# A hybrid layer step: the samples' attention emitted in parts among the last prompt attention blocks

## The chip, the cores and the metric

The kernel runs on one core of one Trainium2 chip. The metric is the device time of one execution in microseconds (us). The kernel before takes 3902.06 us, the median of three runs (3898.70 to 3906.07). TensorE is called PE here, VectorE DVE, ScalarE ACT, GpSimd POOL and SyncE SP; SP issues all the loads and stores that this text speaks of, in its own order. Each engine works through its instructions in order.

## What is computed

The reference is one decoder layer on a prompt of 2048 tokens and on 8 samples that each bring one new token and 1024 past keys, held in pages of 128. Half of the heads are a gated delta rule; the other half are attention over the 256 keys that an indexer ranks highest. What the change touches is the samples' attention, cut here to its core:

```python
ik_past = cache_ik[page_table].reshape(b, past, IDX_DIM)
ik_all = jnp.concatenate([ik_past, ik], axis=1)
dots = jnp.einsum('bqhd,bsd->bqhs', iq, ik_all)
score = jnp.einsum('bqh,bqhs->bqs', iw, jax.nn.relu(dots))
_, idx = lax.top_k(score, 256)
ks, vs = # keys and values at idx, from the pages or the new token
s = jnp.einsum('bqgrd,bqkgd->bqgrk', qg, ks) * d ** -0.5
p = jax.nn.softmax(jnp.where(valid, s, -jnp.inf))
o = jnp.einsum('bqgrk,bqkgd->bqgrd', p, vs)
```

There are 4 query heads on 2 key heads of 128, and 8 index heads of 64. The prompt's attention is the same with its own causal keys, in 16 blocks of 128 queries. Then follow an output projection, a residual, and an FFN of SwiGLU form, for prompt and samples.

## The kernel before

The prompt is worked in four groups of 512 tokens. A first phase projects all groups and runs the delta rule. The second, `groups` (L1183 ff.), holds the rest of the attention and the FFN: prompt attention of blocks 4 to 11, `ffn(0)`, copies of the samples' pages into flat buffers in DRAM, the samples' delta rule, prompt attention of blocks 12 to 15, `ffn(1)`, `sample_steps`, `ffn(2)`, `ffn(3)`. That is the order in which the program emits its work. A scheduler with a timeline then sets the order on each engine, so work that is emitted early and is ready fills in among other work; the order of two users of one rotating buffer stays as emitted. A second branch of the program with a general selection is there too and is not taken in the profiled execution.

**FFN.** `ffn` of a group (512 tokens) runs `rowb`/`rows_s` (L1332, L1343: rows of the modulation spread by PE), the output projection, and the two FFN products, all by `mm3` (L157 to L159: three passes over numbers split in a high and a low part). It reads the attention's output `oT_d` from DRAM as `ca` (L1370). `ffn(3)` also carries the 8 samples: their attention output `oTs` becomes the stack `hs` (L166, L167), which the projection uses by `mm_s` (L173, L174). So `ffn(3)` cannot go past its projection's first half before prompt blocks 12 to 15 and the samples' attention are done.

**Prompt attention** (`attend`). For each of two key heads and each 512 keys it loads `kT`, makes a score matmul S per query head (L1289) into a PSUM buffer of tag "s" (two buffers), and DVE adds the selection's bias and takes the maximum (L1290). Two exponentials on ACT follow (L1296). Then, for every two blocks of keys, one step: four transposes T (L1308) into a PSUM buffer of tag "g" (two buffers, the accumulator `po` holds one), a copy by ACT (L1311) to `PT`, and two matmuls PV with the values (L1314). The output goes to `oT_d` (L1323). `index` before it makes the index scores on PE (L1246) and `select` searches for the threshold: ten passes of ACT (L1145, Sign with a count) with a DVE step after each.

**The samples' attention** (`sample_steps`). Indexer: per sample 8 transposes of index keys (L1039), two matmuls of 8 rows (L1043), relu, two matmuls with the head weights (L1045); `select` on 8 rows. Scores: per sample a load of 1 MB of keys (L1065) into the tile `big`, shared with the prompt attention; per key head and half four transposes (L1070), an ACT copy, and a matmul of 32 rows by 512 (L1073), in which only the rows of that sample are not zero, so that all samples accumulate in one PSUM tile per half. L1075 adds the selection's mask. After the softmax on 32 rows come 8 transposes (L1088), and the product with the values, AV: per sample a load of 1 MB (L1100) and 8 matmuls (L1107). A "matmul" on float32 is two PE instructions in the profile.

Of the kernel before, what the change touches and what calls it, by code (L numbers as in the profile page):

```python
# [34 lines left out]
NS = 8  # L35
# [20 lines left out]
WR, WI = 2, 3  # L56

# [4 lines left out]
def const_tables():  # L62
# [19 lines left out]
    s32 = np.zeros((128, 32), np.float32)  # L82
    for kv in range(2):
        for s in range(8):
            for r in range(2):
                s32[s, kv * 16 + s * 2 + r] = 1.0
    parts["s32"] = s32
    d32 = np.zeros((128, 8), np.float32)
    d32[:32] = s32[:8, :].T
    parts["d32"] = d32  # L90
    parts["pw"] = np.tile((0.5 ** np.arange(1, SEARCH + 1)).astype(np.float32), (128, 1))
    parts["io"] = np.tile(np.arange(16, dtype=np.float32), (128, 1))
    off, cols = {}, 0
    for k, v in parts.items():
        off[k] = (cols, v.shape[1])
        cols += v.shape[1]
# [8 lines left out]
CF, COFF, CL = const_tables()  # L105


class K:
# [84 lines left out]
    def build(self):  # L193
        tc, nc = self.tc, self.nc
        with ExitStack() as es:
# [10 lines left out]
            self.ikp_d = self.dr.tile([NS, 128, NPAGE, 64], F32, name="ikp_d")  # L206
# [14 lines left out]
    def consts(self):  # L221
# [4 lines left out]
        cf = self.cf = cp.tile([128, CF.shape[1]], F32, name="cf")  # L226
# [3 lines left out]
        def c(k):  # L230
            o, n = COFF[k]
            return cf[:, o:o + n]
# [7 lines left out]
        self.s32 = c("s32")  # L240
        self.d32 = c("d32")
# [13 lines left out]
        self.iqTs = cp.tile([64, NS, 8], F32, name="iqTs")  # L255
        self.ikTs = cp.tile([128, NS], F32, name="ikTs")
# [10 lines left out]
    def modulation(self):  # L267
# [34 lines left out]
        nc.sync.dma_start(self.cf[:, 128:], A["cf"][:, 128:])  # L302
# [128 lines left out]
    def copy_pages(self):  # L431
# [5 lines left out]
        for dst, src in ((self.ikp_d, A["cache_idx_k"][0]), (self.kp_d, A["cache_k"][0].rearrange("g t h d -> g t (h d)")),  # L437
                         (self.vp_d, A["cache_v"][0].rearrange("g t h d -> g t (h d)"))):
            for s in range(NS):
                for g in range(NPAGE):  # L440
                    with tc.manual_schedule(engines={nc.sync.engine}):
                        i = s * NPAGE + g
                        pg = nc.sync.value_load(pt_i[0:1, i:i + 1], min_val=0, max_val=n_phys - 1)
                        nc.sync.dma_start(dst[s, :, g, :], src[ds(pg, 1)].rearrange("a t c -> (a t) c"))
# [78 lines left out]
    def narrow(self, g, smT, samp):  # L523
# [59 lines left out]
        for t in range(nb):  # L583
# [6 lines left out]
            if t == 4:  # L590
                nc.sync.dma_start(O[9][0, :, 0, :], ik[:NS, 0, :])
                pk = self.ps.tile([128, 512], F32, name="d", tag="d", bufs=4)
                nc.tensor.transpose(pk[:64, :NS], ik[:NS, 0, :], self.id[:NS, :NS])
                nc.scalar.copy(self.ikTs[:64], pk[:64, :NS])
# [46 lines left out]
    def tok(self, what, blk, pd, rows):  # L641
# [45 lines left out]
        else:  # L687
            self.rope(a[R].rearrange("p (h d) -> p h d", h=8), self.ri, blk, rows, 8, 8, "ropei")
            if samp:
                for h in range(8):  # L690
                    nc.tensor.transpose(pt[:64, h * rows:(h + 1) * rows], a[R, h * 64:(h + 1) * 64], self.id[R, R])
                nc.scalar.copy(self.iqTs.rearrange("p n h -> p h n"), pt[:64, :64].rearrange("p (h n) -> p h n", h=8))
# [197 lines left out]
    def sample_gdn(self):  # L890
        nc, p, A, O = self.nc, self.p2, self.A, self.O
        raws = self.raws
        tl, at = p.tile([128, 832], F32, name="gs", bufs=1), [0]
# [10 lines left out]
        def big():  # L904
            return p.tile([128, 512], F32, name="gS", tag="gS", bufs=2)
# [85 lines left out]
    def sample_steps(self, general):  # L991
# [4 lines left out]
        def P():  # L996
            return self.ps.tile([128, 512], F32, name="g", tag="g", bufs=2)

        def P2():
            return [self.ps.tile([128, 512], F32, name="s", tag="s", bufs=2) for _ in range(2)]  # L1000

        def big():
            return q.tile([128, T], F32, name="big", tag="big", bufs=2)

        def mid():
            return q.tile([128, 512], F32, name="PT", tag="PT", bufs=2)

        b0 = q.tile([128, T + 18], F32, name="sc", tag="sc", bufs=2)
        wk, pr = b0[:NS, 0:NK], b0[:32, NK + 16:2 * NK + 16]
        b = q.tile([128, 512], F32, name="oT", tag="oT", bufs=OB)  # L1010
        PT = b[:, 0:256].rearrange("p (g r) -> p g r", g=NPAGE)
        b = b[:, 256:]
        iwT, ws, nw, dg, pnT, st = b[:8, 0:8], b[:8, 8:72], b[:8, 72:88], b[:32, 88:96], b[:NS, 96:128], b[:32, 128:131]
        qk = b[:, 132:164]

        pw = P()
        nc.tensor.transpose(pw[:8, :8], self.iw[:NS, 16, :], self.id[:NS, :NS])
        nc.vector.tensor_copy(iwT, pw[:8, :8])
        nc.vector.memset(ws, 0.0)
        nc.vector.tensor_copy(ws[:, 0:64:9], iwT)  # L1020

        pw = P()
        for s in range(NS):
            nc.tensor.matmul(pw[:8, s:s + 1], self.iqTs[:, s, :], self.ikTs[:64, s:s + 1], start=True, stop=True)
        nc.scalar.activation(nw[:, 0:8], pw[:8, :8], AF.Relu)
        nc.vector.tensor_tensor(nw[:, 0:8], nw[:, 0:8], iwT, op=OP.mult)
        pw = P()
        nc.tensor.matmul(pw[:NS, 0:1], nw[:, 0:8], self.ones[:8, 0:1], start=True, stop=True)
        nc.vector.tensor_copy(wk[:, PAST:NK], pw[:NS, 0:1])
        psc = P2()  # L1030
        for s in range(NS):
            ikp = mid().rearrange("p (g c) -> p g c", g=NPAGE)
            nc.sync.dma_start(ikp, self.ikp_d[s])
            b = big()
            ikT, rl = b[:64, 0:1024], b[:8, 1024:2048]
            for a in range(2):
                pt = P()
                for g in range(4):
                    nc.tensor.transpose(pt[:64, g * 128:(g + 1) * 128], ikp[:, a * 4 + g, :], self.id)  # L1039
                nc.scalar.copy(ikT[:, a * 512:(a + 1) * 512], pt[:64])  # L1040
            for a, (c0, c1) in enumerate(CH):
                pd = P()
                nc.tensor.matmul(pd[:8], self.iqTs[:, s, :], ikT[:, c0:c1], start=True, stop=True)  # L1043
                nc.scalar.activation(rl[:, c0:c1], pd[:8], AF.Relu)
# [462 lines left out]
```

## Time and profile before

| what | us |
|---|---|
| median of three runs | 3902.06 |
| lowest, highest | 3898.70, 3906.07 |
| the profiled execution | 3907.43 |
| its span | 3905.6 |
| PE busy | 3622.6 |
| DVE busy | 2198.6 |
| ACT busy | 1558.2 |
| POOL busy | 637.6 |

The profile is of one execution. The granted clock of PE over the whole is 0.969 of full speed. In the rows of the profile a name such as `PE s L1073 x2` is the engine, the tile written, the line of the kernel before, and how many instructions. Groups of instructions give the form, the count, then the busy time in us and the mean of one in ns, then the idle time of the engine before them and who ended it. PEld is the load of weights into PE, which overlaps with its matmuls.

### The profile page before, as it was taken

How to read it: one execution, taken by the hardware profiler on the slowest of the kernel's cores; microseconds unless marked ns; L12 is line 12 of the kernel's file. 1: busy time of each engine (PE TensorE's matmuls, PEld its weight loads, DVE VectorE, ACT ScalarE, POOL GpSimd, SP SyncE). 2: the span in 40 equal slices, each digit the busy share in tenths (PEclk: the TensorE clock that was granted, in tenths of full speed). 3: DMA queues.
4: the chain of work that ended last, by engine and by line, in shares of the span. 5: the costliest groups of instructions: out<-in, count | busy, mean ns of one | idle time of the engine just before them, and what ended most of it. 6: DMA issues, size and time to landing. Idle time of an engine off the chain costs nothing.

```text
span 3905.6 us, 50899 instructions
## 1 busy us (share of the span) xinstructions
PE 3622.6 (93%) x17420; PEld 2821.4 (72%) x17420; DVE 2198.6 (56%) x4456; ACT 1558.2 (40%) x2979; POOL 637.6 (16%) x534
## 2 busy tenths in 40 slices
PE   8898988899899899999999999999999999889996
PEld 4777877788777777777766787776777764567775
DVE  3556545553665656766677667667665333244444
ACT  2333223333333433544456545534653335122322
POOL 0000000010000111111131211342121112112223
PEclk9899999999999999999999999999999999999998
DMA  6663454374456434455444333334333325332222
GB/s 237 218 232 115 141 194 135 125 236 143 146 170 212 133 103 144 118 161 159 125 152 130 99 94 102 104 113 156 113 92 110 94 90 187 112 103 82 81 82 68
DMA packets 371872, 528.21 MB, mean 135 GB/s; under 512 B 46036, under 2 KB 250873, under 8 KB 369546
## 3 DMA queue, kind: packets, MB, share of 16 engines
q1 hardware_dynamic: 371602, 524.86, 41.8%
q8 instruction: 139, 2.28, 0.2%
q14 instruction: 131, 1.07, 0.1%
HBM read 427.33 MB, written 116.36 MB: 139 GB/s over the span
## 4 chain that ended last, share of the span: by engine, by line
PE 69%; DVE 12%; DMA 7%; issue 5%; ACT 4%; POOL 1%; SPq 1%; ACTq 0%; DVEq 0%; POOLq 0%
PE d L157 16%; PE d L158 16%; PE d L159 16%; PE s L1246 3%; PE g L1314 2%; PE g L809 2%; DVE wi L142 2%; PE g L814 1%; PE s L1289 1%; PE g L738 1%; DMA wi<-kept 1%; PE g L1308 1%; ACT bias L1145 1%; ACT wi L141 1%; PE g L173 1%
## 5 line engine op out<-in xcount | busy, mean ns | idle before, releaser
L142 DVE TENSOR_TENSOR wi<-wr,wi 128x512 fp32r<-128x512 f32 x712 | 525.4, 744 | 705.4 <-ACT wi L141 695.0
L141 ACT CAST wi<-wr 128x512 fp32r<-128x512 f32 x712 | 437.9, 619 | 926.9 <-PE d L159 331.6
L157 PE MATMUL d<-hh,wi 128*128 128x512 f32 x1792 | 728.1, 408 | 14.8 <-DVE th L1433 5.6
L158 PE MATMUL d<-hl,wi 128*128 128x512 f32 x1792 | 708.1, 395 | 0.0
L159 PE MATMUL d<-hh,wi 128*128 128x512 f32 x1792 | 658.2, 397 | 0.7 <-DVE wi L142 0.7
L1363 POOL TENSOR_TENSOR xt<-xt,tm 128x512 f32<-128x512 f32 x224 | 332.8, 1503 | 588.7 <-DVE tm L1362 504.0
L157 PEld LDWEIGHTS d<-hh,wi 128*128 128x128 f32 x1792 | 339.0, 189 | 103.0 <-DVE th L1433 7.2
L159 PEld LDWEIGHTS d<-hh,wi 128*128 128x128 f32 x1792 | 337.2, 189 | 79.8 <-issue 7.2
L158 PEld LDWEIGHTS d<-hl,wi 128*128 128x128 f32 x1792 | 339.2, 189 | 71.1 <-issue 6.2
L157 PE MATMUL d<-wi,hh 128*128 128x512 f32 x768 | 299.1, 410 | 15.1 <-DMA wi<-kept 10.8
L158 PE MATMUL d<-wi,hh 128*128 128x512 f32 x768 | 304.3, 396 | 0.0
L159 PE MATMUL d<-wi,hl 128*128 128x512 f32 x768 | 303.1, 396 | 0.0
L157 PE MATMUL d<-wi,ah 128*128 128x512 f32 x704 | 268.0, 414 | 15.8 <-DVE tm L1362 11.1
L158 PE MATMUL d<-wi,ah 128*128 128x512 f32 x704 | 281.5, 401 | 0.0
L1439 POOL TENSOR_TENSOR al<-ca,ah 128x512 fp32r<-128x512 f32 x88 | 122.5, 1407 | 938.7 <-ACT ah L1438 935.7
L159 PE MATMUL d<-wi,al 128*128 128x512 f32 x704 | 275.1, 402 | 0.0
L1255 DVE SCALAR_TENSOR_TENSOR sc<-rl,iw,sc 128x512 f32<-128x512 f32 (+3 forms) x224 | 177.9, 794 | 75.7 <-ACT rl L1248 67.4
L1145 ACT ACTIVATE bias<-sc,sv 128x640 bf16<-128x640 f32 (+12 forms) x130 | 181.2, 1394 | 69.1 <-DVE sv L1143 35.7
L1248 ACT ACTIVATE rl<-s 128x512 f32<-128x512 f32 (+3 forms) x288 | 147.8, 543 | 120.0 <-PE s L1246 82.7
L1362 DVE TENSOR_TENSOR tm<-d,row 128x512 f32<-128x512 f32 x224 | 150.6, 684 | 77.7 <-POOL xt L1363 38.2
L157 PEld LDWEIGHTS d<-wi,hh 128*128 128x128 f32 x768 | 146.2, 191 | 53.3 <-DMA wi<-kept 13.6
L157 PEld LDWEIGHTS d<-wi,ah 128*128 128x128 f32 x704 | 132.6, 190 | 59.3 <-issue 10.8
(489 smaller groups left out, 5881.1 us busy)
## 6 DMA issues: line engine op xcount, KB each, us to landing
wr<-in_w_ffn_in_dram SPq DMA_DIRECT2D x704, 128.0 KB, 2.2
wi<-kept SPq DMA_DIRECT2D x168, 512.0 KB, 3.4
wr<-in_w_ffn_out_dram SPq DMA_DIRECT2D x176, 256.0 KB, 2.7
kept<-wi SPq DMA_DIRECT2D x56, 512.0 KB, 3.3
xt<-in_x_prompt_dram SPq DMA_DIRECT2D x8, 2048.0 KB, 8.0
wr<-in_w_ada_dram SPq DMA_DIRECT2D x64, 256.0 KB, 3.3
wr<-in_w_out_dram SPq DMA_DIRECT2D x64, 256.0 KB, 2.9
wr<-in_w_in_dram SPq DMA_DIRECT2D x56, 256.0 KB, 3.4
```

Of the source, the lines that this page charges most:

```text
L141: nc.scalar.copy(w[:, 0], wr)
L142: nc.vector.tensor_tensor(w[:, 1], wr, w[:, 0].bitcast(F32), op=OP.subtract)
L157: nc.tensor.matmul(out, wh, xh, start=start, stop=False, **kw)
L158: nc.tensor.matmul(out, wh, xl, start=False, stop=False, **kw)
L159: nc.tensor.matmul(out, wl, xh, start=False, stop=stop, **kw)
L1145: nc.scalar.activation(c, s, AF.Sign, bias=t, accum_out=cnt)
L1246: nc.tensor.matmul(ps[:, :w], iq[:, h, :].bitcast(F32R), B["ikT"][c * 2 + a][:, :w].bitcast(F32R), start=a == 0, stop=a == 1)
L1248: nc.scalar.activation(r[:, :w], ps[:, :w], AF.Relu)
L1255: nc.vector.scalar_tensor_tensor(s, r[:, :w], iw, s, op0=OP.mult, op1=OP.add)
L1362: nc.vector.tensor_tensor(tm[:rows], pd[:rows], rw, op=OP.mult)
L1363: nc.gpsimd.tensor_tensor(xt, xt, tm[:rows], op=OP.add)
L1439: nc.gpsimd.tensor_tensor(al[b], a, ah[b].bitcast(F32), op=OP.subtract)
```

## The change

`sample_steps` becomes a generator. It stops at a `yield` after the selection, after the first half of the scores (keys 0 to 511 of each sample's pages), after the softmax, and at its end; `attn(range(12, 16))` resumes it once ahead of each of the four blocks, so the four resumptions run the indexer with its selection, the first half of the scores, the second half with the softmax, and the product with the values. Its call between `ffn(1)` and `ffn(2)` is gone.

It also gets buffers of its own: `s2` (eight of 128 x 512 numbers), `s4` (two) and `sb`, rather than the prompt attention's `big`, `PT`, `sc`, `oT`, `iqT`, `qT` and `bias`; `select` uses its own small tiles for it. PSUM stays shared. `keys()` loads one piece of 256 KB, transposes it in four and copies it by ACT. The indexer takes samples in pairs (two index keys of 64 stacked on 128 rows; `iqB`, `ikP` and `ikp_d` are laid out for that). Score matmuls write one of four groups of 32 PSUM partitions (`ps[j*32:...]`), by key head and by sample of a pair; the AV matmuls write the group of their page modulo four, with 32 loads of 256 KB for 8 of 1 MB, and a matmul with `f4` adds the four groups up. The samples' delta rule takes `s2` and `s4` for its own scratch tiles. Rope tables move to a tile of the first phase. The core of the diff:

```diff
+S2, S4, DYN = 8, 1044, 1024
...
-            self.ikp_d = self.dr.tile([NS, 128, NPAGE, 64], F32, name="ikp_d")
+            self.ikp_d = self.dr.tile([NS // 2, 128, NPAGE, 2, 64], F32, name="ikp_d")
...
-        def big():
-            return q.tile([128, T], F32, name="big", tag="big", bufs=2)
...
+        def s2():
+            return q.tile([128, 512], F32, name="s2", tag="s2", bufs=S2)
...
+        def keys(src):
+            kp, kT, pt = s2().rearrange("p (g c) -> p g c", g=4), s2(), P()
+            nc.sync.dma_start(kp, src)
+            for g in range(4):
+                nc.tensor.transpose(pt[:, g * 128:(g + 1) * 128], kp[:, g, :], self.id)
+            nc.scalar.copy(kT, pt)
+            return kT
...
+        for a, (c0, c1) in enumerate(CH):
+            kT = [keys(self.ikp_d[n, :, a * 4:a * 4 + 4].rearrange("p g e c -> p g (e c)")) for n in range(4)]
+            ps = P("s")
+            for n in range(4):
+                nc.tensor.matmul(ps[n * 32:n * 32 + 32], self.iqB[:, n, :], kT[n], start=True, stop=True)
+            nc.scalar.activation(rl[:, c0:c1], ps, AF.Relu)
+            pw = P()
+            nc.tensor.matmul(pw[:NS], ws, rl[:, c0:c1], start=True, stop=True)
+            nc.vector.tensor_copy(wk[:, c0:c1], pw[:NS])
...
+        yield
...
-                    nc.tensor.matmul(pss[a][:32], qp[:, kv, s, :], kT, start=s == 0 and kv == 0, stop=False)
...
+            ps = P("s")
+            nc.tensor.matmul(ps, self.s128[:NS, :], wk[:, c0:c1], start=True, stop=False, skip_group_check=True)
+            for n in range(4):
+                kT = [keys(self.kp_d[n * 2 + j % 2, :, a * 4:a * 4 + 4, j // 2 * 128:j // 2 * 128 + 128]) for j in range(4)]
+                for j in range(4):
+                    nc.tensor.matmul(ps[j * 32:j * 32 + 32], qp[:, j // 2, n * 2 + j % 2, :], kT[j], start=False, stop=n == 3, skip_group_check=True)
+            nc.scalar.copy(pr[:, c0:c1], ps)
+            if a == 0:
+                yield
...
+        yield
...
-            nc.sync.dma_start(vp, self.vp_d[s])
...
+            for g2 in range(4):
+                vp = s2().rearrange("p (g c) -> p g c", g=2)
+                nc.sync.dma_start(vp, self.vp_d[s, :, g2 * 2:g2 * 2 + 2])
+                for b in range(2):
+                    g = g2 * 2 + b
+                    j = slice(g % 4 * 32, g % 4 * 32 + 32)
+                    nc.tensor.matmul(po[j, :256], z[:, g, :], vp[:, b, :], start=s == 0 and g < 4, stop=False, skip_group_check=True)
...
+            nc.tensor.matmul(pt[:, kv * 32:(kv + 1) * 32], o[:, kv * 128:(kv + 1) * 128], self.f4, start=True, stop=True)
...
+        yield
...
-        self.attn(range(12, 16), B, general)
+        part = self.sample_steps(general)
+        self.attn(range(12, 16), B, general, None, part)
         self.ffn(1)
-        self.sample_steps(general)
         self.ffn(2)
...
-    def attn(self, blocks, B, general, then=None):
+    def attn(self, blocks, B, general, then=None, part=None):
 
         for j, i in enumerate(blocks):
+            if part is not None:
+                next(part)
```

How this moves instructions is shown at three places; lines are those of the kernel concerned. The first is PE just ahead of the samples' first projection matmul (L173 before, L176 after). Before, there stand the last score matmul L1073, the mask L1075, the softmax's small matmuls and the whole AV product L1107:

```order
L1073 MATMUL s<-PT,qT 32x512
L1075 MATMUL s<-sc,cf 32x512
L1078 MATMUL g<-sc,cf 32x1
L1079 MATMUL g<-ones,oT 32x1
L1073 MATMUL s<-PT,qT 32x512
L1075 MATMUL s<-sc,cf 32x512
L1088 MATMUL g<-cf,sc 128x32 x8
L1092 MATMUL g<-cf,oT 8x32
L1107 MATMUL s<-big,iqT 32x256 x64
L1108 MATMUL s<-vs,oT 32x256
L1113 MATMUL g<-cf,PT 128x32 x2
L173 MATMUL g<-wi,hs 40x512
```

After, the same stretch holds prompt attention of blocks 14 and 15 (S is L1315, T is L1334, PV is L1340, the rows' factors L1345), with the samples' transposes (L1106, L1111) and AV (L1130) between:

```order
L1315 MATMUL s<-kT,qT 128x384 x2
L1334 MATMUL g<-cf,big 128x128 x4
L1340 MATMUL g<-PT,V 128x256 x2
L1334 MATMUL g<-cf,big 128x128 x4
...
L1345 MATMUL g<-cf,st 128x128 x2
L1106 MATMUL g<-cf,s_21798 128x128 x8
L1111 MATMUL g<-cf,sb 8x128
L1130 MATMUL s<-s_23156,s_23151 32x256 x2
L1315 MATMUL s<-kT,qT 128x512
...
L1345 MATMUL g<-cf,st 128x128 x2
L176 MATMUL g<-wi,hs 40x512
```

Between the first rows of `ffn(3)` (L1332 before, L1358 after) and that projection matmul PE has, beside 36 output-projection matmuls in both, before the samples' scores and AV, and after 116 transposes, 60 PV and 22 S of the prompt attention, and AV.

The second place is PE among the FFN matmuls, where the samples' indexer stood in `ffn(2)` before:

```order
L1043 MATMUL g<-big,iqTs 8x512
L157 MATMUL d<-hh,wi 128x512
L158 MATMUL d<-hl,wi 128x512
L1045 MATMUL s<-big,oT 8x512
L1039 MATMUL g<-cf,PT 64x128 x4
```

After, the samples' scores stand among the FFN and index matmuls (L160 to L162, L1272): one score matmul L1088 and the four transposes of the next piece L1035, then FFN matmuls until the next:

```order
L160 MATMUL d<-wi,ah 128x512
L1088 MATMUL s<-s_21891,s_21783 32x512
L1272 MATMUL s<-ik_12041,iqT 128x512
L1272 MATMUL s<-ik_12043,iqT 128x512
L161 MATMUL d<-wi,ah 128x512
L162 MATMUL d<-wi,al 128x512
L1035 MATMUL g<-cf,s_21899 128x128 x4
L160 MATMUL d<-wi,ah 128x512
```

The 32 score matmuls stand singly in this way; no two of different column groups are neighbours there.

The third place is SP. Before, the loads of the samples' keys and values end the attention's loads, and the weights of `ffn(3)` follow:

```order
L1065 DMA big<-kp_d 128x2048
L1479 DMA out_dram<-xt 128x1024 x4
L1065 DMA big<-kp_d 128x2048
L1366 DMA xt<-in_x_prompt_dram 128x4x1024
L1065 DMA big<-kp_d 128x2048 x6
L1100 DMA big<-vp_d 128x2048 x8
L140 DMA wr<-in_w_out_dram 128x512 x11
```

After, all loads of the samples' values (L1126) stand behind the store of block 14's output (L1349), and the store of block 15's output stands ahead of the last loads of `ca` (L1396):

```order
L1349 DMA oT_d<-oT 128x4x128
L1126 DMA s_23156<-vp_d 128x512
...
L1126 DMA s_23306<-vp_d 128x512
L1311 DMA kT<-kT_d 128x512
L1330 DMA V<-V_d 128x4x128 x5
L1349 DMA oT_d<-oT 128x4x128
L143 DMA wr<-in_w_out_dram 128x512
L1396 DMA ca<-oT_d 128x512 x2
```

What moved is the last part of the samples' keys, out of this place, and the end of the prompt attention, into it.

More of the change, by code (lines that the diff above doesn't have):

```diff
@@ L93, in const_tables @@
     off, cols = {}, 0
+    for k in ("ra", "ri"):
+        parts[k] = parts.pop(k)
     for k, v in parts.items():
@@ L231, in c @@
             o, n = COFF[k]
-            return cf[:, o:o + n]
+            return cf[:, o:o + n] if o < NC0 else self.cr[:, o - NC0:o - NC0 + n]
         self.id = c("id")
@@ L592, in narrow @@
                 pk = self.ps.tile([128, 512], F32, name="d", tag="d", bufs=4)
-                nc.tensor.transpose(pk[:64, :NS], ik[:NS, 0, :], self.id[:NS, :NS])
-                nc.scalar.copy(self.ikTs[:64], pk[:64, :NS])
+                nc.vector.tensor_copy(ik[:NS, 1, :], ik[:NS, 0, :])
+                nc.tensor.transpose(pk[:, :NS], ik[:NS].rearrange("p a c -> p (a c)"), self.id[:NS, :NS])
+                for e in range(2):
+                    nc.scalar.copy(self.ikP[e * 64:e * 64 + 64], pk[e * 64:e * 64 + 64, e:NS:2])
                 continue
@@ L1019, in sample_steps, with P @@
-        nc.vector.memset(ws, 0.0)
-        nc.vector.tensor_copy(ws[:, 0:64:9], iwT)
-        pw = P()
[L1023 to L1026, printed above, removed]
+        def P(tag="g"):
+            return self.ps.tile([128, 512], F32, name=tag, tag=tag, bufs=2)
+        def s2():
+            return q.tile([128, 512], F32, name="s2", tag="s2", bufs=S2)
@@ L1027, in sample_steps @@
         pw = P()
-        nc.tensor.matmul(pw[:NS, 0:1], nw[:, 0:8], self.ones[:8, 0:1], start=True, stop=True)
+        nc.tensor.matmul(pw[:NS, 0:1], ws, rl[:, PAST:NK], start=True, stop=True)
         nc.vector.tensor_copy(wk[:, PAST:NK], pw[:NS, 0:1])
[L1030 to L1044, printed above, removed]
-                nc.tensor.matmul(psc[a][:NS], ws[:, s * NS:(s + 1) * NS], rl[:, c0:c1], start=s == 0, stop=s == NS - 1)
@@ L1096, in sample_steps @@
+        PZ = s2().rearrange("p (x g c) -> p x g c", x=2, g=NPAGE)
         nc.gpsimd.memset(PZ, 0.0)
-        po = P2()[0]
+        po = P("s")
         for s in range(NS):
-            vp, z = big().rearrange("p (g c) -> p g c", g=NPAGE), PZ[:, s % 2]
-            nc.sync.dma_start(vp, self.vp_d[s])
-            rows = lambda w, n: w[:, :, n * 2:n * 2 + 2], lambda w, n: w[:, :, 16 + n * 2:18 + n * 2]
-            for row in rows:
+            z = PZ[:, s % 2]
+            for kv in range(2):
+                c = lambda n: slice((kv * 2 + n % 2) * 8 + n // 2 * 2, (kv * 2 + n % 2) * 8 + n // 2 * 2 + 2)
@@ L1103, in sample_steps @@
                 if s >= 2:
-                    nc.gpsimd.memset(row(z, s - 2), 0.0)
-                nc.gpsimd.tensor_copy(row(z, s), row(PT, s))
-            for g in range(NPAGE):
-                nc.tensor.matmul(po[:32, :256], z[:, g, :], vp[:, g, :], start=s == 0 and g == 0, stop=False)
-        nc.tensor.matmul(po[:32, :256], pnT, self.vs[:NS, :], start=False, stop=True)
-        o = mid()[:32, :256]
-        nc.scalar.copy(o, po[:32, :256])
+                    nc.gpsimd.memset(z[:, :, c(s - 2)], 0.0)
```

155 lines of the change are left out of this document (82 added, 73 removed).

## The prediction

> **What bounds the kernel now.** I read the page's busy times and the chain's shares first, then the windows of all engines over the three stretches that the change touches, then the chain in order of time in the last of them.
>
> ```profile
> span 3905.6 us, 50899 instructions
> PE 3622.6 (93%) x17420; PEld 2821.4 (72%) x17420; DVE 2198.6 (56%) x4456; ACT 1558.2 (40%) x2979; POOL 637.6 (16%) x534
> PE 69%; DVE 12%; DMA 7%; issue 5%; ACT 4%; POOL 1%; SPq 1%; ACTq 0%; DVEq 0%; POOLq 0%
> ```
>
> TensorE (PE) is busy 93% of the span and carries 69% of the chain, so what counts is PE time, and the places where PE has nothing else to do. The windows (columns: stretch and its length, then busy time of PE, PEld, DVE, ACT and POOL, granted clock, DMA share, GB/s) cover the FFN of groups 1 and 2, the stage with the samples' attention, and the last FFN:
>
> ```profile
> 2672.00:3251.40 579.40, 567.71 (x2463) 425.71 (x2461) 303.45 (x551) 265.95 (x435) 119.56 (x104) 0.98 0.33 102
> 3251.40:3365.50 114.10, 102.41 (x414) 43.41 (x413) 32.41 (x71) 38.22 (x73) 11.99 (x36) 0.96 0.53 189
> 3365.50:3905.60 540.10, 486.90 (x2116) 370.69 (x2116) 239.00 (x344) 156.74 (x295) 136.43 (x112) 0.95 0.27 83
> ```
>
> In the first stretch PE is busy 567.7 of 579.4 us: work put there costs its PE time, work taken out gives it back. The second, 114.1 us, is the **end stage**: `ffn(3)`'s first rows and 36 output-projection matmuls are all that the FFN can offer; the rest is the samples' attention alone. The chain in order of time (start, us, what) gives PE's unit prices:
>
> ```profile
> 3095.50 0.86 PE s L1289 x2
> 3116.52 0.86 PE g L1314 x4
> 3123.70 0.44 PE g L1308 x4
> 3169.52 0.56 PE g L1039 x4
> 3173.77 0.95 PE g L1043 x2
> 3180.70 0.95 PE s L1045 x2
> 3251.42 0.58 PE d L1332 x4
> 3265.21 0.92 PE g L1070 x7
> 3271.35 0.97 PE s L1073 x2
> 3272.32 0.59 PE g L1070 x4
> ```
>
> So for prompt attention: a score matmul S costs .86 (two instructions), four transposes T .44, the PV matmuls of one step .86. For the samples: four index transposes .56, an indexer matmul or head-weight matmul .95, four key transposes .59, a score matmul .97.
>
> **The change, part by part.** *The samples' indexer and scores* move from the end stage and the end of `ffn(2)` into the FFN of groups 1 and 2. Before, 8 samples cost 16 x (.56 + .95 + .95) = 39.4 us for the indexer, of which two index-transpose groups, 2.5 matmuls L1043 and 4 L1045 (7.3 us) stood after the end stage's start: 32.1 inside the FFN. After, 40 `keys()` pieces cost 40 x .59 = 23.6, 10 indexer and head-weight matmuls 9.5, 32 score and two mask matmuls 34 x .97 = 33.0: 66.1. So **+34.0**. The score matmuls write four column groups, but the order shows them one at a time with some 20 FFN matmuls between, so each is costed whole. The 40 copies that `keys()` puts on ACT, at the .59 of the copy row below 23.6 us, replace 16 of the indexer and 32 of the scores and lie where ACT is busy 266 of 579 us; uncovered they would cost no more than that.
>
> The Trainium skill ("TensorEngine Tiling (Array Packing)", Theoretical Speedup) gives up to 4x for outputs of 32 columns or fewer. If that held, the 32 score matmuls would cost 8 us and not 31, and the sum fall by 23; that needs neighbours in four groups, which the order doesn't have. No run here shows it.
>
> *The prompt attention pushed out*: between `ffn(3)`'s first rows and the samples' first projection matmul now stand 29 T, 30 PV steps' pairs and 22 S of blocks 14 and 15, which used to lie in the FFN. They leave it: 29 x .44 + 30 x .86 + 22 x .86 less .4 for two short S = 57.1, so **-57.1**. First stretch: 34.0 - 57.1 = **-23.1** (within -28, if its 11.7 idle us shrink by 5, and -18, if they grow so).
>
> *The end stage after.* Nothing covers this attention, so it runs at the pace of its own loop. Rows of the timeline, where the same loop lay in the FFN, and of the groups of instructions there:
>
> ```profile
> 3117.22 0.60 PE L1308 MATMUL g<-cf,big 128*128 128x128 f32 x4
> 3117.86 0.59 ACT L1311 COPY PT<-g 128x512 f32<-128x512 f32 x1 [2.38 <-PE g L1308]
> L1290 DVE CUSTOM_DVE_ANT_0 big<-s,bias,st 128x512 f32<-128x512 f32 x28 | 20.8, 747 | 8.3 <-PE s L1289 8.1
> L1296 ACT ACTIVATE big<-big,st 128x2048 f32<-128x2048 f32 x4 | 8.0, 2004 | 5.5 <-DVE st L1295 5.5
> L1296 ACT ACTIVATION_READ_ACCUMULATOR big<-big,st 128x1 f32 x12 | 2.2, 185 | 0.0
> L1145 ACT ACTIVATE bias<-sc,sv 128x2048 bf16<-128x2048 f32 x10 | 20.0, 2001 | 2.7 <-DVE sv L1143 1.5 <-DVE sv L1147 1.2
> ```
>
> The order has T, PV, T, PV strictly in turn, with ACT's copy between T and its PV: a step takes .60 + .04 + .59 + .05 + .86 = 2.14 us, of which PE waits .68. Between a half's last S and its first T stand two exponentials, 2 x (2.0 + .19) = 4.4, in which PE has nothing; with six S still to run, 5.2, a bubble of 9.6. What the clock does in such places is shown by PE's windows of 3.41 us (stretch, length, PE busy, clock):
>
> ```profile
> 2080.06:2083.47 3.41, 1.76 (x7) 1.00 0.08 26
> 2083.47:2086.89 3.42, 2.60 (x6) 0.50 0.25 77
> 2086.89:2090.30 3.41, 3.02 (x6) 0.50 0.02 6
> 2090.30:2093.71 3.41, 3.41 (x6) 0.50 0.94 285
> 2093.71:2097.12 3.41, 2.53 (x8) 1.00 1.03 417
> 2714.93:2718.35 3.42, 2.76 (x8) 0.50 0.90 372
> ```
>
> After a window busy 1.76 of 3.41 the clock is halved; windows busy 2.60, 2.76 and 3.02 leave it at half; only a full one, 3.41, restores it. A bubble with 4.4 us of idle PE halves it. At half clock a step takes 1.30 more (.44 and .86 doubled), 3.44, and PE is busy 2.76 of it, 80%, or 2.74 of a window: not full. So the half stays slow to its end.
>
> The Trainium skill ("TensorE: Matmul & The Clock Gate", What's actually happening) says that the clock is throttled after at least one idle window of about 3.4 us and released after one busy window. Read as "mostly busy", it would release the clock in the second window of each half. The rows at 2.60 to 3.02 us speak against that reading; what it would give is rival B.
>
> For the samples' part:
>
> ```profile
> L1107 PE MATMUL s<-big,iqT 128*32 128x256 f32 x128 | 31.1, 405 | 5.5 <-DMA big<-vp_d 4.6 <-POOL iqT L1105 0.9
> 3355.69 7.07 PE L1107 MATMUL s<-big,iqT 128*32 128x256 f32 x32 [1.45 <-DMA big<-vp_d]
> 3260.00:3270.00 10.00, 10.00 (x46) 1.00 0.87 325
> V<-V_d SPq DMA_DIRECT2D x54, 256.0 KB, 2.8
> oT_d<-oT SPq DMA_DIRECT2D x12, 256.0 KB, 3.1
> ca<-oT_d SPq DMA_DIRECT2D x32, 256.0 KB, 3.7
> ```
>
> The AV matmuls: 128 instructions at 7.07 / 32 = .221 are 28.3 us one after the other, 14 if two column groups run side by side; nothing in the trace shows which. All 32 loads of past values stand on SP behind block 14's store `oT_d<-oT`, so 8 MB come in during the stage: at 325 GB/s 25.8 us, after a first landing of 2.8. Bounds 28 and 37 (28.3, seven S between them at .86, half clock at the start); I take 31, nearest to the loads.
>
> Sum of the end stage: rows and projection (13.8 from L1332 to L1070, less the indexer's 7.3, plus four steps at 1.30) 12; block 14's first half, 2.5 steps of 2.14, plus block 15's Sign passes of 2.0 + .19 that the order puts between its copies (six, half of them under the projection), 3: 8.4; bubble 9.6; second half 7.5 x 3.44 = 25.8; the samples' transposes 3.4 (the page's .59 and .97 with two copies); AV 31; block 15's first half, eight steps 17.1 (its S and exponentials lie under AV); bubble 9.6; second half 8 x 3.44 = 27.5; last copy and store-off 1.2. Together 145.6, against 114.1: **+31.5**.
>
> *Behind it*: block 15's store and reload are now last: 3.1 + 3.7, a cast and a subtraction of some 2, less the samples' projection matmuls and 12 others that stand ahead (about 5): **+4** (0 to 9). *The rest*: new constants and two loads of them, the index rope's stacking, page copies in pairs, the new tiles of the samples' GDN stage lie in stretches where PE has other work and are a handful of instructions: 0, at most 2 if uncovered.
>
> Sum: -23.1 + 31.5 + 4 = **+12.4**. The profiled execution took 3907.4 (1.8 outside its span), 5.3 over the median 3902.1. 3907.4 + 12.4 = 3919.8; with the same 5.3 taken off, **3914**.
>
> **The rivals.**
>
> *A2, one half keeps the clock.* If block 15's second half follows AV at full clock and its bubble is shorter than a window, 8 x 1.30 = 10.4 is not paid: 3904, no change. For it: its bubble may straddle two windows. Against: 4.4 us is longer than one.
>
> *B, both keep it.* 15.5 x 1.30 = 20.2 less: 3894, on the other side. The mechanism is a clock that a window at 80% restores; it decides as soon as the second window of a half is at 1.00. Against it stand the 3.02 and 2.76 rows.
>
> *C, and the groups overlap.* B, plus AV at the loads' pace 28 and the -28 in the FFN: 3894 - 3 - 5 = 3886. Against: both need several favourable bounds.
>
> *D, SP's line.* In the FFN the 40 `keys()` loads of 256 KB stand on SP between the weight loads, each waiting for a buffer that PE frees; what stands behind is the next weights. The nearest row is the AV wait of 4.6 us over eight loads, .6 each: 32 waits make 19, and the time 3933. Against: eight buffers, and PE's idle 11.7 us in that stretch although its V loads wait likewise.
>
> That the change doesn't do what it says (parts left where they were) is excluded by the order.
>
> **How the numbers follow.** 0.2% (7.8 us) is about what a measurement can tell from no change: 3894.3 to 3909.9. Chances: the forecast .47, A2 .17, B .20, C .06, D .10. Faster: C .06, two thirds of B .13, .06 from the forecast and A2 with the lower bounds of AV, tail and FFN together (5 + 4 + 5): .25. Slower: the forecast .34, D .10, A2 .03: .47. The rest is .28. The range leaves out half of D and most of C: low 3885, high 3934.
>
> **What would show it.** Right: a stage of about 146 us between the first rows of `ffn(3)` and the samples' first projection matmul, with clock .50 in two of its attention halves, steps of 3.4 us there; the FFN ahead some 23 us shorter. Wrong: steps of 2.1 throughout (B); PE idle in the FFN on `wr` loads (D); score matmuls below .97 each; a stage that is under 125 us.

## The result, and the profile after

The changed kernel takes 3951.73 us (median of four runs, 3949.03 to 3961.01), the kernel before, in runs beside it, 3902.95: a ratio of 1.0126, 95% interval 1.0113 to 1.0140. It is slower by 49 us where 12 were forecast, and lies above the range. Measured again beside the experiments (their run five) it stood at 3937.28 to 3896.97, a ratio of 1.0106 (1.0089 to 1.0123).

The page's first lines of the changed kernel, in its profiled execution of 3961.01 us (the slowest of the four):

```profile
span 3959.1 us, 50815 instructions
PE 3619.8 (91%) x17338; PEld 2814.6 (71%) x17338; DVE 2208.6 (56%) x4457; ACT 1548.8 (39%) x2965; POOL 633.5 (16%) x528
```

PE's busy time is that of before within 3 us, while the span is 53.5 longer, so in sum PE is idle for longer. (A matmul at half clock counts as busy for twice as long, so the sum alone doesn't tell waiting from a slow clock.) Where it lies is seen by windows between the same points of the program: block 13's index or the FFN matmul beside it, the first rows of `ffn(3)`, the samples' first projection matmul, the end. Before:

```profile
2412.60:3251.40 838.80, 814.75 (x3645) 624.97 (x3643) 471.61 (x890) 381.11 (x633) 210.32 (x161) 0.98 0.35 109
```

(its two later windows stand in the prediction: 114.1 and 540.1 us), and after:

```profile
2421.20:3245.10 823.90, 791.98 (x3493) 594.85 (x3492) 456.85 (x837) 355.63 (x604) 206.89 (x149) 0.98 0.37 112
3245.10:3418.10 173.00, 125.52 (x485) 72.53 (x483) 50.14 (x118) 52.19 (x78) 11.12 (x38) 0.76 0.34 110
3418.10:3959.10 541.00, 488.65 (x2116) 371.07 (x2116) 242.92 (x345) 159.31 (x299) 139.28 (x116) 0.95 0.27 85
```

Up to 2412.6 and 2421.2 the two profiles differ by 8.6 us, where both kernels do nearly the same; other kernels of this study, which are alike up to there, lie between 5.0 less and 6.5 more than before at that point, so this part is mostly the spread between executions; that none of it is the change's is not shown. The FFN stretch is 14.9 us shorter, the end stage **58.9** longer, the rest .9: together 53.5. In the end stage PE's mean clock is .76, and it is busy 126 of 173 us. The same stage cut by its parts (first half of block 14 with the rows; bubble; second half; the samples' transposes; AV; first half of block 15; bubble; second half):

```profile
3245.08:3271.46 26.38, 19.42 (x101) 1.00 0.57 208
3271.46:3286.34 14.88, 8.09 (x17) 0.74 0.28 88
3286.34:3316.99 30.65, 23.10 (x62) 0.50 0.08 24
3316.99:3322.69 5.70, 2.18 (x9) 0.50 0.84 209
3322.69:3358.93 36.24, 29.04 (x150) 0.90 0.75 243
3358.93:3377.65 18.72, 13.61 (x72) 1.00 0.19 56
3377.65:3385.80 8.15, 5.84 (x14) 1.00 0.11 32
3385.80:3418.15 32.35, 24.25 (x67) 0.53 0.03 9
```

Both second halves run at half clock. PE's waits in the stage (line, who ended the wait, us in total, times, the longest):

```profile
PE g L1340 <- ACT PT L1337: 21.6, 28, 1.3
PE s L1130 <- DMA s<-vp_d: 9.5, 8, 3.5
PE g L1334 <- ACT big L1322: 9.1, 4, 3.8
PE s L1315 <- DVE st L1316: 4.3, 5, 2.1
```

The 21.6 us are the copy between T (L1334) and its PV (L1340), 28 times. The timeline shows a step of it at half clock, and one at full:

```profile
3293.50 2.08 PE L1340 MATMUL g<-PT,V 128*128 128x256 f32 x4 [0.73 <-ACT PT L1337]
3295.37 1.06 PE L1334 MATMUL g<-cf,big 128*128 128x128 f32 x4
3297.16 2.08 PE L1340 MATMUL g<-PT,V 128*128 128x256 f32 x4 [0.73 <-ACT PT L1337]
...
3362.68 1.13 PE L1340 MATMUL g<-PT,V 128*128 128x256 f32 x4 [0.73 <-ACT PT L1337]
3363.65 0.60 PE L1334 MATMUL g<-cf,big 128*128 128x128 f32 x4
3364.98 1.13 PE L1340 MATMUL g<-PT,V 128*128 128x256 f32 x4 [0.73 <-ACT PT L1337]
```

From PV to PV it is 3.66 us (3297.16 - 3293.50) and 2.30 us. And why the attention of blocks 14 and 15 stands here at all begins 800 us earlier: the rows of block 13's index matmuls (durations in ns, then the first and the last start), of before and of after:

```profile
L1246 PE MATMUL s<-ik,iqT x64: 277/393/486, 2414.9 to 2490.7; 128*128 128x512 f32 x48, 128*128 128x256 f32 x16
```

```profile
L1272 PE MATMUL s<-ik,iqT x64: 277/389/583, 2622.8 to 2698.7; 128*128 128x512 f32 x48, 128*128 128x256 f32 x16
...
L1272 PE MATMUL s<-ik,iqT x64: 333/392/500, 2782.6 to 2951.2; 128*128 128x512 f32 x48, 128*128 128x384 f32 x16
```

After the change block 13's index starts 208 us later (the first row), among the last score matmuls of the samples' indexer (2605.7 to 2628.9 us), and block 14's (the second row) takes 169 us.

### The profile page after: what moved, and what is told of

Read it like the earlier page. It is cut to its first block, busy times and chain, and to the rows that moved or that the text cites. A ratio compares the mean times of both kernels' runs of the same rounds, so it can differ in the third digit from the quotient of the medians.

```text
span 3959.1 us, 50815 instructions
## 1 busy us (share of the span) xinstructions
PE 3619.8 (91%) x17338; PEld 2814.6 (71%) x17338; DVE 2208.6 (56%) x4457; ACT 1548.8 (39%) x2965; POOL 633.5 (16%) x528
## 3 DMA queue, kind: packets, MB, share of 16 engines
q14 instruction: 131, 1.07, 0.1%
## 5 line engine op out<-in xcount | busy, mean ns | idle before, releaser
L160 PE MATMUL d<-hh,wi 128*128 128x512 f32 x1792 | 729.6, 408 | 17.0 <-DMA wi<-kept 5.4
L162 PE MATMUL d<-hh,wi 128*128 128x512 f32 x1792 | 655.9, 397 | 0.7 <-DVE wi L145 0.7
L160 PEld LDWEIGHTS d<-hh,wi 128*128 128x128 f32 x1792 | 339.0, 189 | 108.6 <-issue 8.6
L162 PEld LDWEIGHTS d<-hh,wi 128*128 128x128 f32 x1792 | 337.7, 189 | 83.1 <-issue 9.5
L160 PE MATMUL d<-wi,hh 128*128 128x512 f32 x768 | 296.2, 407 | 18.3 <-DMA wi<-kept 12.0
L162 PE MATMUL d<-wi,hl 128*128 128x512 f32 x768 | 300.2, 394 | 0.0
L160 PE MATMUL d<-wi,ah 128*128 128x512 f32 x704 | 266.5, 411 | 17.7 <-DVE tm L1388 13.1
L162 PE MATMUL d<-wi,al 128*128 128x512 f32 x704 | 276.4, 401 | 0.0
L1169 ACT ACTIVATE bias<-sc,sv 128x640 bf16<-128x640 f32 (+11 forms) x120 | 169.7, 1414 | 60.8 <-DVE sv L1171 29.3
L160 PEld LDWEIGHTS d<-wi,hh 128*128 128x128 f32 x768 | 145.9, 191 | 55.3 <-DMA wi<-kept 15.1
L1272 PE MATMUL s<-ik,iqT 128*128 128x512 f32 (+3 forms) x576 | 163.9, 387 | 15.2 <-ACT rl L1274 11.2
```

The source lines that it names most:

```text
L160: nc.tensor.matmul(out, wh, xh, start=start, stop=False, **kw)
L162: nc.tensor.matmul(out, wl, xh, start=False, stop=stop, **kw)
L1169: nc.scalar.activation(c, s, AF.Sign, bias=t, accum_out=cnt)
L1272: nc.tensor.matmul(ps[:, :w], iq[:, h, :].bitcast(F32R), B["ikT"][c * 2 + a][:, :w].bitcast(F32R), start=a == 0, stop=a == 1)
```

## The experiments

Two theories were put against each other first: the loss is the *place* (parts ahead of blocks push prompt attention out of the FFN's cover, where its steps are serial), or it is the *new code* of the samples' attention wherever it stands. Times are medians, each beside the kernel before on the same chip.

**One: the new code in the old place.**

```diff
-        self.attn(range(12, 16), B, general, None, part)
+        self.attn(range(12, 16), B, general)
         self.ffn(1)
+        for _ in part:
+            pass
```

> The changed kernel with all parts of the samples' attention emitted in one piece between ffn(1) and ffn(2), as before; the new tiles, pieces and column groups stay. Theory 1 (the loss is the place: parts ahead of blocks 12 to 15 push the prompt attention out of the FFN's cover): prompt attention of block 15 ends near 3160 us again, the end stage holds 27 pieces x .59 + 32 scores x .97 + 12 of rows and projection + about 8 of softmax + 6 of transposes + 36 of AV = 109 against 114 before, and the FFN ahead saves some 15: 3884, at any rate below 3910. Theory 2 (the new code is slow wherever it stands: single pieces of 256 KB, four-way sums): 3930 or more. If two column groups ran side by side, the scores would cost a fraction of .97 each and the time be nearer 3870.

Measured 3929.73 to 3894.73, a ratio of 1.0086 (1.0069 to 1.0103). Theory 1 missed its number by far (3884), and the forecast of the second theory (3930 or more) came true: the new code loses in the old place too. The prompt attention ends near 3160 us as the first theory said, but the end stage takes 147.2 us, where 109 were expected. In 12.0 of them PE waits, ahead of the first score, for the selection's mask, which the new code adds first. Then come the pieces; the timeline, at half clock and then at full (L1035 the transposes of a piece, L1088 its score):

```profile
3292.47 1.11 PE L1035 MATMUL g<-cf,s 128*128 128x128 f32 x4
3294.26 1.91 PE L1088 MATMUL s<-s,s 128*32 128x512 f32 x2 [0.68 <-ACT s L1036]
3296.11 1.11 PE L1035 MATMUL g<-cf,s 128*128 128x128 f32 x4
...
3325.61 1.05 PE L1088 MATMUL s<-s,s 128*32 128x512 f32 x2 [0.72 <-ACT s L1036]
3326.59 0.66 PE L1035 MATMUL g<-cf,s 128*128 128x128 f32 x4
3327.96 1.05 PE L1088 MATMUL s<-s,s 128*32 128x512 f32 x2 [0.72 <-ACT s L1036]
```

Each score stands straight behind its own transposes and waits for their copy: 3.64 us a piece, 2.35 at full clock, where before the change the transposes of the next piece came first and a piece took 1.56 (.59 and .97). It is the same defect as in the prompt attention, in another loop.

**Two: the parts behind the blocks.**

```diff
-            if part is not None:
-                next(part)
...
             self.attend(i, B, self.biases.pop(i))
+            if part is not None:
+                next(part)
```

> The changed kernel with each part emitted behind the attention of a block (12 to 15), not ahead of it. Theory 1 (the order of the shared PSUM buffers delays the prompt attention): block 13's index matmuls start near 2415 us as before the change and not at 2623; the end stage holds block 15 alone, nine pieces and AV, about 132 against 173, and the FFN ahead takes back some 16: 3927. Theory 2 (the new code's own cost): no change from 3952.

Measured 3914.25 to 3894.73, 1.0046 (1.0029 to 1.0063). Block 13's index starts at 2417 us, and the end stage is 143.4, with block 15 alone and the last scores in it, at up to 3.64 us a piece. Against the second theory: the same new code, put elsewhere, is 23 us faster than the changed kernel's 3937.28 (by the two ratios as well), where theory 1 had 25. So each theory holds a part: the place costs, and so does the new code.

**Three: a second PSUM buffer for the transposes of blocks 14 and 15.**

```diff
-                pt = self.ps.tile([128, 512], F32, name="g", tag="g", bufs=2)
+                tg = "s" if i >= 14 and b0 % 4 else "g"
+                pt = self.ps.tile([128, 512], F32, name=tg, tag=tg, bufs=2)
```

> The changed kernel, but in blocks 14 and 15 every second set of four transposes goes to a PSUM buffer of tag s and not g, so that the next transposes can run while ACT copies. Theory of the end stage (its steps are serial, T, copy, PV, at 2.30 us, and 3.66 where the clock is halved): steps of about 1.4 us, clock back at 1.00, 15 x 2.26 + 15 x .9 = 47 us less: 3905. Rival (ACT's copies, the loads of values or the exponentials set the pace): less than 10 us gained, above 3940.

Measured 3899.26 to 3894.73, 1.0008 (.9998 to 1.0018): by the two ratios 38 us of the changed kernel's 41 are gone (47 were expected), though the attention still stands where it did. The timeline shows transposes ahead of the PV before them, no wait, a step in 1.30 us:

```profile
3265.26 0.60 PE L1335 MATMUL g<-cf,big 128*128 128x128 f32 x4
3265.70 1.03 PE L1341 MATMUL g<-PT,V 128*128 128x256 f32 x4
3266.57 0.60 PE L1335 MATMUL s<-cf,big 128*128 128x128 f32 x4
3267.00 1.03 PE L1341 MATMUL g<-PT,V 128*128 128x256 f32 x4
```

The end stage falls to 119.6 us at a mean clock of .96. So the exposed attention costs little as such; its serial steps and the clock that they let fall cost it.

**Four: the clock alone.** Repeated PV matmuls fill PE's wait. They share a PSUM tile with the sums of blocks 14 and 15, which they change.

```diff
+                if i >= 14 and b0 >= 2:
+                    for b in range(2):
+                        nc.tensor.matmul(po[:, 256:], V[:, b, :], PT[:, b * 256:(b + 1) * 256], start=True, stop=True, skip_group_check=True)
                 PT = B["PT"]()
```

> The changed kernel, but in blocks 14 and 15 each step repeats two PV matmuls of the step before into the unused half of its PSUM tile, between T and PV; they add PE work of .86 us a step where PE waits .73. Nothing reads them. Theory (the second halves are slow because PE is not busy throughout a window, so the clock stays at .50): with PE always busy the clock returns to 1.00 in the second window, steps there fall from 3.66 to about 2.5, 15 steps gain 17 and the others lose 2: 3937. Rival (the clock stays down for another reason): each step there grows by 1.0, the others by .1, about 3968.

Measured 3939.49 to 3894.73, 1.0110 (1.0091 to 1.0128): no gain over the changed kernel. In the trace the mechanism shows: PE's window is full, and in the one after it the filled steps take 2.30 us at full clock (3293.95 on). But block 14's first half grew to 30.0 us by the filler, and in the changed kernel's second profile (run five) the clock returned in block 14's second half without it. So the whole time is no price of the clock. One half is: block 15's second half was at half clock in both profiles of the changed kernel (32.35 and 31.56 us); with the filler the clock comes back in its second step and the half takes 23.2 us (3375.56 to 3398.80), 8 to 9 less, behind the same bubble of 8.15.

**Five: the changed kernel again.**

> The changed kernel itself, beside the experiments on one chip. From the ratio so far (1.0126) it should stand 49 us above the kernel before there. Only its place among the experiments is asked: the first FFN stretch some 14 us shorter, the end stage near 173 us.

Measured 3937.28 to 3896.97, 1.0106: 40 us above the kernel before, where 49 were expected. Its stage took 161.6 us in this profile (173 were expected), and the FFN stretch is 11 shorter than before. Of the 11.4 us between the two profiles' stages, 8.0 are block 14's second half: 22.7 and not 30.65.

**Six: two and three together.**

> Both edits that won time, together: parts behind the blocks, and every second set of transposes of blocks 14 and 15 in a tag-s buffer. If the losses are the two named (prompt attention pushed out of the FFN, and its serial steps where it stands uncovered), the end stage holds block 15 alone at about 1.5 us a step, one or two pieces and AV: about 92 against 114 before, and the FFN stretch is some 15 shorter: 35 to 40 us below the kernel before, a ratio near .991. If the gains are one and the same (the second takes away what the first would have), it stays near the pipelined kernel alone, a ratio of 1.000.

Measured 3882.93 to 3896.97, .9963 (.9949 to .9977): 14 us below the kernel before, not 35 to 40. The stage is as expected (89.3 us, expected 92); the FFN stretch is 833.1 us from block 13's index to the first rows of `ffn(3)`, before 836.5, so it gained 3 and not 15, since block 14's attention lies in it again. The two together are 28 us shorter in the profiles and 14 in the medians; the profiled execution of the kernel before was itself 10 above its median here (3907.43 and 3896.97), and where in it those lie isn't known.

**Seven: the old place, keys loaded into a shared tile of 1 MB.**

The parts stand where they stand in run one, and `keys` takes its piece from the loaded tile. The core of the edit:

```diff
-                kT = [keys(self.kp_d[n * 2 + j % 2, :, a * 4:a * 4 + 4, j // 2 * 128:j // 2 * 128 + 128]) for j in range(4)]
+                big = q.tile([128, T], F32, name="big", tag="big", bufs=2).rearrange("p (e g c) -> p e g c", e=2, g=4)
+                for e in range(2):
+                    nc.sync.dma_start(big[:, e], self.kp_d[n * 2 + e, :, a * 4:a * 4 + 4, :])
+                kT = [keys(None, big[:, j % 2, :, j // 2 * 128:j // 2 * 128 + 128]) for j in range(4)]
```

> The kernel with the parts in the old place, but the samples' keys loaded as two halves of 512 KB into one shared tile of 1 MB, not as four single pieces of 256 KB in the ring of eight. Theory (its 35 us over the kernel before come from scores that stand straight behind their own transposes, 2.35 us a piece and 3.65 at half clock, because the ring lets a load start only when a score ends): transposes run ahead of the scores, the scores stand in groups and side by side, 25 pieces take about 30 us and not 78, 45 us less than the kernel in the old place, about .997 of the kernel before. Rival (the loss is in the four-way sums, the selection's wait or AV): less than 10 us gained.

Measured 3889.01 to 3896.97, .9976 (.9965 to .9986): 41 us less than in run one. Transposes run ahead and scores stand in twos (L1093 is the score):

```profile
3281.84 1.05 PE L1093 MATMUL s<-s,s 128*32 128x512 f32 x4
3282.83 0.66 PE L1037 MATMUL g<-cf,big 128*128 128x128 f32 x4
3283.41 1.04 PE L1093 MATMUL s<-s,s 128*32 128x512 f32 x2
```

Two scores of different column groups (x4) take no longer than one (x2), and four pieces take 5.1 us (3278.28 to 3283.41), 1.28 each. PE still waits 9.3 us for the selection's mask ahead of the first score, so that wait isn't the difference. The loss of run one was its order, and the small loads in the ring of eight made it; the edit changes the ring and the size of the loads at once, so which of the two did it is not shown.

**Eight: the second PSUM buffer in the kernel before.** The edit of run three.

> The kernel before with the second PSUM buffer for the transposes of blocks 14 and 15. There its attention lies under FFN matmuls, so its steps are not serial on PE. Theory: no gain beyond 0.2% from the steps themselves; PE's work only moves, so within 10 us of the kernel before. Rival (the second buffer is a gain by itself, wherever it stands): 40 us or more below it, as it gave in the changed kernel.

Measured 3895.56 to 3896.97, .9998 (.9989 to 1.0007): nothing, as forecast: there FFN matmuls stand between those steps.

**Nine: one emission swapped.** Block 13's index ahead of the first part.

```diff
-            if part is not None:
+            if part is not None and j > 0:
                 next(part)
...
+            if part is not None and j == 0:
+                next(part)
             self.attend(i, B, self.biases.pop(i))
```

> The changed kernel with one emission swapped: the index of block 13 ahead of the first part, not behind it; the other parts stay ahead of their blocks. Theory (part one, which waits for the samples' delta rule until near 2600 us, holds up block 13's index by the order of the shared buffers, and all prompt attention after it): block 13's index starts near 2417 us and not 2610, block 14's attention fits under the FFN, the end stage holds block 15 and AV at 120 against 173, the FFN takes back 19: 34 us less, about 3903 where the changed kernel has 3937. Rival (the delay comes later, from the scores' accumulator that holds one of two tag-s buffers): less than 10 us gained.

Measured 3890.21 to 3894.95, .9991 (.9981 to 1.0002): 47 us less than the changed kernel's 3937.28, by one swap, where 34 were expected. Its rows of the index of blocks 13 and 14, and its stage:

```profile
L1274 PE MATMUL s<-ik,iqT x64: 274/393/487, 2421.3 to 2497.2; 128*128 128x512 f32 x48, 128*128 128x256 f32 x16
...
L1274 PE MATMUL s<-ik,iqT x64: 333/391/776, 2715.1 to 2868.3; 128*128 128x512 f32 x48, 128*128 128x384 f32 x16
```

```profile
3251.58:3352.80 101.22, 74.70 (x372) 0.97 0.49 164
```

Block 13's index is back at 2421, while block 14's still takes 153 us; the stage is 101 (expected 120). So the delay of the first index is what cost; the accumulator of scores that holds one of two tag-s buffers (the rival) slows the next index, but it isn't needed to explain the loss.

**Ten and eleven: all indexes ahead of the parts, then with the second buffer.**

```diff
             if n is not None:
                 self.index(n, B, general)
+            if part is not None:
+                next(part)
             self.attend(i, B, self.biases.pop(i))
```

> The same swap for all four parts: each block's successor is indexed ahead of the part, the part stands between index and attention. Theory: the index runs at full pace, AV and all samples' work come under the FFN, and only the second half of block 15 stays uncovered: 36 output-projection matmuls and rows 12, a bubble of 9, eight steps of 3.66 at half clock 29, 5 around them, 55 against 114 before, while the FFN stretch grows by the PE work that now lies in it, some 40 more than before: 15 to 20 us below the kernel before, a ratio of .995 to .996. Rival (the 32 single loads on SP between weight loads make PE wait once AV too lies there): no gain, the FFN's idle time up by 15 or more.

> That swap and the second buffer for the transposes of blocks 14 and 15. Nothing of the attention is left between ffn(3)'s first rows and the samples' projection. What is left to gain is PE's idle time and the dearer of the samples' matmuls: before, PE was busy 917 of 953 us from block 13's index to the samples' projection; with 30 us less of samples' work on PE and an idle share as in the FFN, 32 us, that is 919: 34 us below the kernel before, a ratio of .991. Rival (as in the run before this: waits on loads in the FFN take the gain): .997 or more.

Ten measured 3859.71 to 3894.95, .9919 (.9905 to .9932), eleven 3857.64, .9908 (.9893 to .9923): below both kernels, 35 and 37 us under the kernel before. Eleven is as forecast (34); ten was put at 15 to 20. In ten block 14's index takes 67 us, and the stage 53:

```profile
L1272 PE MATMUL s<-ik,iqT x64: 331/392/775, 2705.0 to 2771.9; 128*128 128x512 f32 x48, 128*128 128x384 f32 x16
```

```profile
2412.75:3263.67 850.92, 830.84 (x3821) 0.99 0.40 124
3263.67:3317.00 53.33, 42.55 (x146) 0.72 0.28 104
```

From block 13's index to the samples' projection it is 904 us, before 953. The stage is as expected (55), but the FFN stretch grew by 12 us and not by 40. It holds all of AV and idles 20 us of 851, before 24 of 839: the loads on SP cost nothing that shows.

**Twelve: AV with one sample's loads.**

```diff
-                vp = s2().rearrange("p (g c) -> p g c", g=2)
-                nc.sync.dma_start(vp, self.vp_d[s, :, g2 * 2:g2 * 2 + 2])
+                if s == 0:
+                    vps.append(s2().rearrange("p (g c) -> p g c", g=2))
+                    nc.sync.dma_start(vps[g2], self.vp_d[s, :, g2 * 2:g2 * 2 + 2])
+                vp = vps[g2]
```

> The changed kernel, but AV loads the values of sample 0 only and uses them for all eight; it leaves out 28 of 32 loads, and the samples' attention output is not the reference's. Theory (AV waits for its loads, and two column groups run side by side where they are there): AV falls from 36 us to about 20, 16 us less in all. Rival (the matmuls run one after the other at .22, 28 us beside 8 S): AV stays at 33 or more.

This leaves out 28 of the 32 loads; the values of sample 0 stand in for all eight. Measured 3924.08 (3914.53 to 3944.01) to 3894.95, 1.0072 (1.0052 to 1.0093): 13 us less than the changed kernel, where 16 were expected. AV takes 14.6 us, from 3315.8 to 3330.4, with four S beside it. Its rows, and two of the changed kernel's AV:

```profile
3322.18 1.93 PE L1132 MATMUL s<-s,s 128*32 128x256 f32 x32
3324.05 1.13 PE L1317 MATMUL s<-kT,qT 128*128 128x512 f32 x2
3325.10 1.93 PE L1132 MATMUL s<-s,s 128*32 128x256 f32 x32
```

```profile
3322.69 1.07 PE L1130 MATMUL s<-s,s 128*32 128x256 f32 x4 [3.52 <-DMA s<-vp_d]
3352.34 1.96 PE L1130 MATMUL s<-s,s 128*32 128x256 f32 x12 [1.39 <-DMA s<-vp_d]
```

32 instructions in 1.93 us are .060 each, against .221 before the change: the four column groups run side by side. So the loads set the pace of the changed kernel's 36 us of AV, but they are not worth 22: the stage is 162.2 us, 10.9 less than in the changed kernel's first profile. The longer AV had covered nine S and the exponentials of block 15's first half; five of those S now come behind it, the clock falls for three steps, and from AV's end to that half's end it is 31.5 us, where it was 18.7.

## Why the prediction was wrong

Its sign, its place and the main of its mechanism (attention that nothing covers, in serial steps, two of its halves at half clock) were right, its size was not: 12.4 us forecast, 53.5 between the profiles and 40 to 49 between the medians.

*The step that failed is the sum of the end stage*: 145.6 forecast, 173.1 measured (161.6 in the second profile). Term by term: first half of block 14 with the rows, 20.4 forecast and 26.4 measured; its bubble 9.6 and 14.9; second half 25.8 and 30.65, a step at 3.66 and not 3.44; the samples' transposes 3.4 and 5.7; AV 31 and 36.2, with nine S in it and not seven; block 15's first half 17.1 and 18.7, a step at 2.30 and not 2.14; its bubble 9.6 and 8.15; its second half with the end 28.7 and 32.35. No one term decides: seven of eight were too small. Three of the causes can be read off.

The first term left matmuls out. The 13.8 us from L1332 to L1070 in the kernel before hold only 20 of the 36 output-projection matmuls; the other 16 stand behind, at 3265.88 to 3269.72, 3.8 us. In the changed kernel rows and projection took 16.4 us (3245.08 to 3261.48), against 12.

The forecast's bubble of block 14 had nothing in it for DVE. There DVE also runs passes of block 15's selection over 2048 numbers, 2.3 us each. S waits until DVE has taken bias and maximum of the S before (L1316), and the exponentials (L1322) wait behind such a pass for the row's maximum:

```profile
3281.45 1.13 PE L1315 MATMUL s<-kT,qT 128*128 128x384 f32 x2 [2.11 <-DVE st L1316]
3281.85 2.29 DVE L1181 MAX8 sv<-sc 128x8 f32<-128x2048 f32 x1
3284.29 1.90 ACT L1322 ACTIVATE big<-big,st 128x1920 f32<-128x1920 f32 x1 [9.29 <-DVE st L1321]
```

The second profile has three such passes and the same kind of waits there, in a bubble of 14.0. Block 15's bubble, with no selection beside it, took 8.15.

The step was priced from rows where FFN matmuls stand between. The hand-overs to ACT and back were put at .09 a step and are .15 at full clock (T from 3363.65, the copy 3364.34 to 3364.92, PV from 3364.98), and from PV's start to the next T it is .97 and not .86.

*The FFN stretch*: PE's busy time there fell by 22.8 us (814.75 to 791.98), where 23.1 were forecast; but its idle time rose by 7.9 (24.05 to 31.92), so the stretch gave 14.9. The bound of 5 us on idle time was too narrow; no single wait makes up the 7.9. The 32 single score matmuls cost about what was forecast (33.5 us of busy time, 31 forecast); they had no neighbours. The Trainium skill's up to 4x for outputs of 32 columns ("TensorEngine Tiling (Array Packing)", Theoretical Speedup) did not come in the scores there, and came where neighbours stood: .221 / .060 is 3.7 in run twelve.

*The tail* was put at 4 and was .9.

*The rivals*: D, loads on SP that stall the FFN, had 19 us; in the changed kernel's FFN stretch PE waits 2.7 us for loads of keys and 1.3 behind late weights, and run ten has still more of them there and no more idle time. A2 did not happen: it named block 15's second half, which was at half clock in both profiles. Nor did B, with both halves at full clock, nor C, which needs it. But block 14's second half regained its clock in the second profile, behind a window busy 2.81 of 3.41 us. So the prediction's reading that only a full window restores the clock did not hold, and that this half stayed slow in the first profile was luck for its forecast.

*What the prediction didn't ask*: why the order had put blocks 14 and 15 there. It took the order as given and priced it, which sufficed for the sign. Run nine shows that the order of emission did it. The way, by the program: buffers of one PSUM tag are handed out as emitted, tag s is the only ring that the first part and an index share, the first part gets to it behind the samples' delta rule (near 2600 us), and block 13's index, ready at 2415, stood behind it. A chain of index, selection and attention that had ended at 3158 us, 93 ahead of the end stage, now ended at 3417.

## What to carry to other kernels

Work that is emitted "in between" takes its turn in every shared ring of buffers: ask of each piece what it waits for, and who comes behind it in the ring, before asking how much it costs. A loop that goes transposes, copy, matmul wants two spare PSUM buffers as soon as nothing else covers it; with one it paid the copy each time here (2.30 us a step against 1.30), and then the clock (3.66). And price a stage that will stand alone from rows that stand alone, hand-overs, half clock and the other engines' work included.

## What the runs showed of the hardware

How busy a window must be for the clock to return stays open. These are PE's windows of 3.41 us, laid where the granted clock changes (stretch, length, PE busy, clock), in the changed kernel's first profile (the first of seven alike, and the one behind them), its second profile, and run four:

```profile
3288.84:3292.25 3.41, 2.68 (x9) 0.50 0.00 0
3312.73:3316.14 3.41, 2.89 (x9) 0.50 0.02 5
```

```profile
3285.59:3289.01 3.42, 2.81 (x8) 0.50 0.00 0
3289.01:3292.42 3.41, 2.56 (x13) 1.00 0.21 58
```

```profile
3290.54:3293.95 3.41, 3.41 (x11) 0.50 0.00 0
```

Windows at 2.68 (79%) did not bring it back, seven in a row; one at 2.81 did, one at 2.89 didn't; a full one did. So PE's busy time in a window, as the profile has it, does not decide alone. The same serial loop near 80% ran a whole half at .50 in one execution and lost two steps only in another, which was 8 us of their difference; that the phase of the windows decides is likely and not shown. The Trainium skill's one busy window ("TensorE: Matmul & The Clock Gate", What's actually happening) agrees with the windows at 2.81 and 3.41, each of which had full clock behind it; that section doesn't say how busy a window must be.

The fall needs no long wait: in the changed kernel's first profile the clock was halved at 3271.77 us, behind a window in which PE was busy 1.66 of 3.41 us and waited 1.07 us at the longest.
